# Hybrid decoder block on one Trainium2 core: block sums of the feed-forward input built with PSUM operands, the ones product four tiles into a unit, weight splits traced behind the norm factor, and the last stores on two queues

## The chip, the cores and the metric

The kernel runs on one core of one Trainium2 chip. The metric is the device time of one execution in microseconds (us). Three runs of the kernel before gave 2236.07, 2233.39 and 2236.08 us, median 2236.07 us. The core has a matrix engine (PE, with its weight loads shown as PEld), a vector engine (DVE), an activation engine (ACT), a general engine (POOL) and a queue engine (SP) that starts most DMA transfers. Each engine works through its own instructions strictly in order and waits on semaphores for the others.

## The reference, cut to what matters

One decoder layer over 1024 tokens and 1024 channels. The change touches the second half of it, the feed-forward block, and the norm ahead of it:

```python
        mixed = (...)                                  # three token mixers, merged by gates
        x = x + rms_norm(mixed @ w_out[l], post_mix_norm[l])
        h = rms_norm(x, pre_ffn_norm[l])               # (1, 1024, 1024)
        u = causal_dwconv(h @ ffn_w_up[l], ffn_conv_w[l], ffn_conv_b[l])   # 2 * 2816 columns, 3 taps
        gate, val = jnp.split(u, 2, axis=-1)
        f = (jax.nn.gelu(gate, approximate=True) * val) @ ffn_w_down[l]
        x = x + rms_norm(f, post_ffn_norm[l])
```

Everything is float32. `rms_norm(x, w)` is `x * rsqrt(mean(x*x) + 1e-6) * w` over the channels.

## The kernel before, in words

**Layout and precision.** Activations lie channel by token: a tile is 128 channels by 512 tokens, and the 1024 tokens form two halves, h = 0 and h = 1. Each float32 operand of a matmul is split into a rounded high part (an ACT copy) and the remainder, a low part (a subtraction on DVE or POOL). One product is three matmuls: high by high, high by low, low by high. A "unit" is 128 output channels for one half: 8 input tiles (k = 0..7) times three matmuls, 24 matmuls into one PSUM bank. PSUM has eight banks here: a pool `psd` of five for products (tile name `dense`) and a pool `psn` of three for everything else.

**Order.** A scheduler orders the instructions of each engine ahead of time by its own time model; what is traced earlier has precedence, and where the code says `keep_in_program_order` or `issue_after` the order is fixed by hand. On the chip each engine keeps that order, whatever arrives late.

**The output projection and the norm (L1334 to L1394).** For each half, eight units of `wo` are added to x and stored (L1363 to L1375). `finish` then makes the input of the feed-forward block: `rstd` (L1348) multiplies the sum of squares `osq` with a matrix of ones (two matmul records into `psn`), and ACT (Ln, Exp) and DVE turn it into a factor. Then eight tiles j are scaled by DVE (L1380), copied by ACT into the high part (L1383) and subtracted into the low part (L1389 on POOL for j = 1, 3, 5 of the second half, otherwise L1391 on DVE). For h = 0 this runs at once. For h = 1 it runs in the middle of the feed-forward block's first units.

**The first four pairs of units (N_FIRST = 4).** `up_first` (L1511) does the eight units u = 0..7 for h = 0. In the last pair (u = 6, 7) `fm_unit` (L273) calls `end` ahead of tile k = NORM_AT = 6 of unit 6: it traces the loads and splits of two further weights (`second`, for u = 0, 1 of the second half) and then `finish` for h = 1. The ones product and the first matmul of tile 6 are kept in program order; unit 7 is free to be put anywhere. The conv of these two units, the gelu (L1611) and the gated product (L1613) are held until tile j = SPLIT_AT = 5 of `finish` has been scaled and split.

`up_second` (L1528) does u = 0..7 for h = 1. For u = 0 and 1 the two units run interleaved tile by tile (L1531 to L1536), because the tiles of h = 1 come one after another out of `finish`. Every unit's weights are 512 KB by DMA into `wraw`, ACT makes the high part `whi` (L269), POOL the low part `wlo` (L270). Up to three such pairs of buffers take turns, so a unit's `whi` waits until the unit three before has been through PE. After each unit follows `conv` (L304): ACT L307 scales PSUM into `u`, ACT L311 does three halo columns, DVE L315 adds two taps; then gelu and, for each pair, the gated product L1503 and its store L1504.

**The block sums (L1577 to L1603).** From the fifth pair on, `up_pair` (L1548) uses a seven-product scheme over 2 by 2 blocks (weights in `weights7`, L1401). Its right-hand sides are sums and differences of the four blocks of h (halves 0 and 1, tiles k and k + 4). `columns` is a generator that `up_second` advances after each unit's conv. Its first four steps call `blocks(k)`: four DVE operations in place on SBUF tiles, `combos` (L1463 to L1466), and two splits (ACT L1591, DVE L1592); the last four steps make two splits each. That is 16 DVE instructions for sums and 16 for low parts. `up_pair` then runs the products in the order 1, 2, 6, 7, 5, 4, 3, each 12 matmuls.

**The end.** The last chunk of the down projection goes over columns 0:512, 512:768 and 768:1024 (`LAST`). `start_norm` (L1842) scales eight tiles by the last norm's factor (L1848), adds x (L1849, on POOL for some tiles, on DVE for the others) and stores each tile from SP (L1850).

Of the kernel before, what the change touches and what calls it, by code (L numbers as in the profile page):

```python
# [10 lines left out]
F32 = mybir.dt.float32  # L11
# [3 lines left out]
OP = mybir.AluOpType  # L15
# [170 lines left out]
SB_SLO = 1  # L186
SB_WLO = 0
H_POOL = (0, 1, 3, 5), (1, 3, 5)
SPLIT_AT = 5
NORM_AT = 6  # L190
T_POOL = (range(8), (0, 1, 2))

T_AT = 3
# [1054 lines left out]
def tail_stage(nc, tc, es, env):  # L1248
# [82 lines left out]
    ow = op.enter_context(tc.tile_pool(name="ow", reuse_waits="tile", bufs=2))  # L1331
    rows = []
    splits = []
    for h in range(2):  # L1334
        o = [x_t(F32) for _ in range(8)]
        rows.append(o)

        def sumsq(sums, src):

            if sums[0] is None:  # L1340
                sums[0] = ow.tile([128, 512], F32, name="osq", bufs=OSQ)
                act(sums[0], src, AF.Square)
            else:
                sq = psn.tile([128, 512], F32, name="psn", tag="psn")
                act(sq, src, AF.Square)
                V.tensor_tensor(sums[0], sums[0], sq, op=OP.add)

        def rstd(ss):  # L1348
            ss, = ss
            ps = psn.tile([128, 512], F32, name="psn", tag="psn")  # L1350
            tc.keep_in_program_order(mm(ps, E.ones, ss, start=True, stop=True))

            V.tensor_scalar(ss, ps, 1.0 / DM, EPS, op0=OP.mult, op1=OP.add)
            act(ps, ps, AF.Ln, scale=1.0 / DM, bias=E.eps)
            act(ps, ps, AF.Exp, scale=-0.5)
            V.tensor_tensor(ss, ss, ps, op=OP.mult)
            V.scalar_tensor_tensor(ss, ss, -0.5, ps, op0=OP.mult, op1=OP.mult)
            V.scalar_tensor_tensor(ps, ss, 1.5, ps, op0=OP.add, op1=OP.mult)
            return ps

        ss = [None]
        for j in range(8):
            ps, = fm_unit(psd, load_w3(A["wo"][j], 1024), lambda k, _: mix[h, k], 8, halves=(h,))  # L1363
            act(o[j], ps, AF.Copy)
            sumsq(ss, ps)
        r = rstd(ss)
        ss = [None]
        for j in range(8):
            x = ow.tile([128, 512], F32, name="ox", bufs=8)
            nc.sync.dma_start(x, A["xT"][j * 128:(j + 1) * 128, hs(h)])  # L1370
            p = psn.tile([128, 512], F32, name="psn", tag="psn")
            V.scalar_tensor_tensor(p, o[j], pvc(PV_PM, j), r, op0=OP.mult, op1=OP.mult)
            V.tensor_tensor(o[j], p, x, op=OP.add)
            sumsq(ss, o[j])
            nc.sync.dma_start(E.x1_d[j * 128:(j + 1) * 128, hs(h)], o[j])  # L1375
        def finish(h=h, o=o, ss=ss, rstd=rstd):
            r = rstd(ss)
            for j in range(9):
                if j < 8:
                    i = V.scalar_tensor_tensor(o[j], o[j], pvc(PV_FFN, j), r, op0=OP.mult, op1=OP.mult)  # L1380
                    tc.keep_in_program_order(i)
                    hi, lo = h2[h, j] = hi_t(), lo_t()
                    a = act(hi, o[j], AF.Copy)  # L1383
                    if j == SPLIT_AT:
                        splits[:] = a, i
                if j > 0:
                    hi, lo = h2[h, j - 1]
                    if j - 1 in H_POOL[h]:
                        P.tensor_tensor(lo, o[j - 1], fl(hi), op=OP.subtract)  # L1389
                    else:  # L1390
                        tc.keep_in_program_order(V.tensor_tensor(lo, o[j - 1], fl(hi), op=OP.subtract))  # L1391

        if h == 0:
            finish()  # L1394
# [63 lines left out]
        act(s, ps, AF.Copy)  # L1458
        return s

    def combos(b11, b12, b21, b22, eng):

        eng.tensor_tensor(b22, b12, b22, op=OP.subtract)  # L1463
        eng.tensor_tensor(b12, b11, b12, op=OP.subtract)
        eng.tensor_tensor(b11, b22, b11, op=OP.subtract)
        eng.tensor_tensor(b21, b11, b21, op=OP.add)  # L1466

    m_d = E.scratch("m_d", [NFF * 128, T])
    ms_d = [E.scratch(f"m{x}_d", [DOWN[-1][0] * 128, T]) for x in ("hi", "lo")]

# [40 lines left out]
    def up_first(f, st, ending=False):  # L1511
        us = 2 * f, 2 * f + 1
        ws = [load_up(u, 0) for u in us]

        def end():
            second.extend(load_up(u, 1) for u in range(2))
            finish()

        for s, u in enumerate(us):
            ps, = fm_unit(psd, ws[s], lambda k, h: h2[h, k], 8, halves=(0,),  # L1520
                          at=(NORM_AT, end) if ending and s == 0 else None)
            with ExitStack() as after:
                if ending:
                    for i in splits:
                        after.enter_context(tc.issue_after(i.ins))
                conv(u, 0, ps, st, gelu=False)

    def up_second(f, st, then):  # L1528
        us = 2 * f, 2 * f + 1
        if f == 0:  # L1530
            pss = [bank() for _ in us]  # L1531
            for k in range(8):
                for (hi, lo), ps in zip(second, pss):
                    s = slice(k * 128, (k + 1) * 128)
                    for n, (a, b) in enumerate(((hi, 0), (hi, 1), (lo, 0))):
                        mm(ps, a[:, s], h2[1, k][b], start=k == 0 and n == 0, stop=k == 7 and n == 2)  # L1536
        for s, u in enumerate(us):
            if f:
                ps, = fm_unit(psd, load_up(u, 1), lambda k, h: h2[h, k], 8, halves=(1,))
            else:  # L1540
                ps = pss[s]
            end = conv(u, 1, ps, st)
            if s == 1:
                gated(f, 1, st)
            with tc.issue_after(end.ins):
                then(u)
# [30 lines left out]
    rhs = {q: [None] * 4 for q in range(1, 8)}  # L1577
    sums = {}

    def blocks(k):  # L1580
        lows = [rows[0][k], rows[1][k], rows[0][k + 4], rows[1][k + 4]]
        combos(*lows, V)
        for q, b in ((1, h2[0, k]), (2, h2[0, k + 4]), (3, h2[1, k + 4])):
            rhs[q][k] = b
        t2, t1, t4, t3 = lows
        sums.update({(6, k): t2, (7, k): t3, (5, k): t1, (4, k): t4})

    def split(q, k, place):
        t = sums[q, k]
        rhs[q][k] = hi, lo = place(), x_t()  # L1590
        act(hi, t, AF.Copy)  # L1591
        V.tensor_tensor(lo, t, fl(hi), op=OP.subtract)  # L1592

    def columns():
        for k in range(4):
            blocks(k)
            split(6, k, x_t)
            split(7, k, x_t)
            yield
        for q, k, place in ((5, 0, hi_t), (5, 2, hi_t), (4, 0, lo_t), (4, 2, lo_t)):  # L1600
            split(q, k, place)
            split(q, k + 1, place)
            yield  # L1603

    first = [{} for _ in range(N_FIRST)]
# [184 lines left out]
    ws = []  # L1790
# [51 lines left out]
    def start_norm(h, s, ss):  # L1842
# [3 lines left out]
        for j in range(8):  # L1846
            a = acc[h][j][:, s]
            V.tensor_tensor(a, a, r[:, :W], op=OP.mult)  # L1848
            (P if j in T_POOL[end] else V).tensor_tensor(a, x1s[h][:, j, s], a, op=OP.add)  # L1849
            nc.sync.dma_start(E.outT[j * 128:(j + 1) * 128, h * 512 + s.start:h * 512 + s.stop], a)  # L1850

    for s0, s1 in LAST:
        h = s0 // 512
# [40 lines left out]
```

## Time and profile before

| What | Before |
|---|---|
| Median of three runs | 2236.07 us (2233.39 to 2236.08) |
| The profiled execution's own time | 2236.53 us |
| Its span, first to last instruction | 2234.8 us |
| PE busy, share of span | 2158.0 us, 97% |
| PEld busy | 1748.4 us, 78% |
| DVE busy | 1361.1 us, 61% |
| ACT busy | 1262.5 us, 56% |
| POOL busy | 1091.7 us, 49% |
| Granted PE clock, mean | 0.988 |
| DMA moved | 240.73 MB, mean 108 GB/s |

Times inside the profile count from the start of the span. A row of the timeline gives start, duration, engine, source line, operation, output and inputs, and in brackets the idle time of the engine just before and what ended it. A window row gives the length of a stretch, then for each engine its busy time and the number of its instruction records in it, then the granted PE clock, the DMA share and GB/s. Successive instructions of an engine overlap a little, so a duration is somewhat larger than the step from one start to the next. Some matmul records are missing from a trace. All matmuls carry line L205, the wrapper that issues them.

### The profile page before, as it was taken

The numbers are of one execution on the slowest core, as the hardware profiler recorded it, in microseconds if no ns is written. First come the engines' busy times: TensorE is split into PE (matmuls) and PEld (weight loads), VectorE is DVE, ScalarE is ACT, GpSimd is POOL, SyncE is SP. The second block draws the span as 40 slices with busy tenths as digits, with TensorE's granted clock in tenths as the row PEclk, the third lists the DMA queues.
The fourth block names the chain that finished last, engine by engine and source line by source line (L and its number), as shares of the span: only waits on it lengthen the run. The fifth ranks groups of instructions, "written<-read, shape, count | busy, mean of one in ns | idle before, by whom it ended". The sixth has DMA issues, their size and how long they took to land.

```text
span 2234.8 us, 30188 instructions
## 1 busy us (share of the span) xinstructions
PE 2158.0 (97%) x10697; PEld 1748.4 (78%) x10697; DVE 1361.1 (61%) x2538; ACT 1262.5 (56%) x2316; POOL 1091.7 (49%) x797
## 2 busy tenths in 40 slices
PE   8999999999999999999999999999989999999997
PEld 7997667667887878777777788888768888888886
DVE  8433784771367677848484443328785666666677
ACT  7144676666476677545555422235556666676574
POOL 3212566576233323434343246445467777765753
PEclk9999999999999999999999999999989999999998
DMA  5223212201111111322223263345334444476533
GB/s 197 83 82 104 57 34 79 64 8 46 49 48 43 53 47 43 113 81 90 95 76 118 78 225 131 106 135 179 118 99 161 160 151 146 141 264 201 186 108 110
DMA packets 127079, 240.73 MB, mean 108 GB/s; under 512 B 29328, under 2 KB 43472, under 8 KB 126928
## 3 DMA queue, kind: packets, MB, share of 16 engines
q1 hardware_dynamic: 126640, 238.58, 32.6%
q8 instruction: 84, 1.38, 0.3%
q14 instruction: 67, 0.55, 0.1%
q10 hardware_dynamic: 288, 0.22, 0.0%
HBM read 179.45 MB, written 59.31 MB: 107 GB/s over the span
## 4 chain that ended last, share of the span: by engine, by line
PE 85%; DVE 8%; ACT 3%; issue 2%; DMA 1%; POOL 1%; SPq 0%; DVEq 0%; ACTq 0%; POOLq 0%
PE dense L205 67%; PE ps_s L205 6%; PE ps_o L205 6%; PE ps_t L205 5%; PE ps_b L205 2%; DVE x L1592 1%; DVE dec L1160 1%; DVE mx L838 0%; DVE x L1848 0%; DVE row L530 0%; ACT wT L862 0%; DVE row L1225 0%; POOL wT_lo L873 0%; ACT h_hi L401 0%; DVE sz L1043 0%
## 5 line engine op out<-in xcount | busy, mean ns | idle before, releaser
L270 POOL TENSOR_TENSOR wlo<-wraw,whi 128x1024 fp32r<-128x1024 f32 (+1 forms) x118 | 270.0, 2290 | 425.7 <-ACT whi L269 423.4
L205 PE MATMUL dense<-h_hi,whi 128*128 128x512 f32 x992 | 400.4, 404 | 10.0 <-DVE row L530 6.3
L205 PE MATMUL dense<-h_hi,wlo 128*128 128x512 f32 x992 | 388.9, 392 | 0.0
L205 PE MATMUL dense<-h_lo,whi 128*128 128x512 f32 x992 | 388.8, 392 | 0.0
L269 ACT ACTIVATE whi<-wraw 128x1024 fp32r<-128x1024 f32 (+1 forms) x118 | 117.9, 999 | 200.6 <-PE dense L205 173.5
L205 PEld LDWEIGHTS dense<-h_hi,whi 128*128 128x128 f32 x992 | 187.4, 189 | 51.1 <-issue 6.6
L205 PEld LDWEIGHTS dense<-h_hi,wlo 128*128 128x128 f32 x992 | 186.7, 188 | 40.7 <-issue 0.8
L205 PEld LDWEIGHTS dense<-h_lo,whi 128*128 128x128 f32 x992 | 187.4, 189 | 34.8 <-issue 0.2
L873 POOL TENSOR_TENSOR wT_lo<-wT,wT_hi 128x512 fp32r<-128x512 f32 x132 | 168.8, 1289 | 87.1 <-ACT wT_hi L872 78.3
L205 PE MATMUL dense<-hi,whi 128*128 128x512 f32 x512 | 201.0, 396 | 8.9 <-ACT whi L1412 4.8
L205 PE MATMUL dense<-lo,whi 128*128 128x512 f32 x512 | 201.7, 394 | 0.3 <-DVE lo L1391 0.3
L205 PE MATMUL dense<-hi,wlo 128*128 128x512 f32 x512 | 199.8, 393 | 0.5 <-POOL wlo L1413 0.4
L1073 POOL TENSOR_TENSOR s_lo<-sa,s_hi 128x512 fp32r<-128x512 f32 (+2 forms) x48 | 53.9, 1126 | 150.7 <-ACT s_hi L1072 141.6
L205 PEld LDWEIGHTS dense<-hi,whi 128*128 128x128 f32 x512 | 97.2, 190 | 31.7 <-ACT whi L1412 5.3
L205 PE MATMUL dense<-x,uhi 128*128 128x512 f32 x360 | 116.7, 389 | 0.0
L205 PEld LDWEIGHTS dense<-hi,wlo 128*128 128x128 f32 x512 | 97.1, 190 | 22.4 <-POOL wlo L1413 1.1
L862 ACT ACTIVATE wT<-ps_s 128x512 f32<-128x512 f32 x132 | 78.5, 595 | 63.6 <-PE ps_s L205 59.2
L205 PEld LDWEIGHTS dense<-lo,whi 128*128 128x128 f32 x512 | 97.2, 190 | 21.8 <-issue 0.7
L315 DVE SCALAR_TENSOR_TENSOR u<-dense,pv,u 128x510 f32<-128x510 f32 (+1 forms) x140 | 101.7, 742 | 8.7 <-ACT u L311 7.5
L872 ACT ACTIVATE wT_hi<-wT 128x512 fp32r<-128x512 f32 x132 | 82.3, 629 | 16.6 <-POOL wT L864 15.1
L205 PE MATMUL ps_s<-Q,K 128*128 128x512 f32 x264 | 83.6, 398 | 4.3 <-DVE Q L849 4.1
L205 PEld LDWEIGHTS dense<-x,uhi 128*128 128x128 f32 x360 | 67.6, 188 | 14.1
(460 smaller groups left out, 5631.9 us busy)
## 6 DMA issues: line engine op xcount, KB each, us to landing
wraw<-in_wfm SPq DMA_DIRECT2D x62, 512.0 KB, 3.7
wraw<-in_wup SPq DMA_DIRECT2D x52, 512.0 KB, 3.8
g_d<-gate_e SPq DMA_DIRECT2D x48, 256.0 KB, 2.0
ge<-g_d SPq DMA_DIRECT2D x24, 512.0 KB, 3.9
m_d<-u SPq DMA_DIRECT2D x44, 256.0 KB, 2.1
u<-m_d SPq DMA_DIRECT2D x36, 256.0 KB, 3.3
wraw<-in_wdn SPq DMA_DIRECT2D x33, 256.0 KB, 3.4
cum<-acum_d SPq DMA_DIRECT2D x32, 256.0 KB, 3.3
```

Of the source, the lines that this page charges most:

```text
L205: i = f(*a, **k)
L269: act(hi, raw, AF.Copy)
L270: (eng or (V if tiles else P)).tensor_tensor(lo, raw, fl(hi), op=OP.subtract)
L315: end = V.scalar_tensor_tensor(o[:, d:], ps[:, :512 - d], taps[d], o[:, d:], op0=OP.mult, op1=OP.add)
L862: act(w.rearrange("p h q -> p (h q)"), pz, AF.Exp)
L872: act(hi, wf, AF.Copy)
L873: P.tensor_tensor(lo, wf, fl(hi), op=OP.subtract)
L1073: (P if SB_SLO else V).tensor_tensor(s_lo[:, c0:], a[:, c0:], fl(s_hi[:, c0:]), op=OP.subtract)
L1160: V.tensor_scalar(dec[:, h, :], cum[:, h, :], E.acum[:, c, 4 * q + h:4 * q + h + 1], 0.0, op0=OP.subtract, op1=OP.min)
L1592: V.tensor_tensor(lo, t, fl(hi), op=OP.subtract)
```

## The change

Four edits; all but the two-queue stores lie between the output projection and the first seven-product pair.

1. `blocks` copies the block b12 into a PSUM tile by ACT (`in_psum`, L1445) and forms two of the four sums in PSUM tiles of `psn`; each of the four DVE operations now has one PSUM input. The splits for products 7 and 6 read those PSUM tiles. For products 5 and 4 each sum is first copied to PSUM by ACT, and the split reads the copy. The fourth operation stays an addition (`b21 = t2 + b21`).
2. The ones product of `finish` for h = 1 is traced at tile 4 of unit 6, not 6, and unit 7 is issued behind it.
3. The two weight loads of `second` with their splits are traced behind the factor (`then` is called after `rstd`), and the conv, gelu and gated product of the last first-half pair are held until tile 7, not 5.
4. The interleaved units 0 and 1 of the second half run tile by tile for k = 0 to 4 only; then unit 0 does k = 5 to 7, and then unit 1. In the last `start_norm` odd tiles are stored from ACT's queue, even ones from SP's.

```diff
-SPLIT_AT = 5
-NORM_AT = 6
+SPLIT_AT = 7
+NORM_AT = 4
...
-            tc.keep_in_program_order(mm(ps, E.ones, ss, start=True, stop=True))
+            summed[0] = mm(ps, E.ones, ss, start=True, stop=True)
+            tc.keep_in_program_order(summed[0])
...
-        def finish(h=h, o=o, ss=ss, rstd=rstd):
+        def finish(h=h, o=o, ss=ss, rstd=rstd, then=None):
             r = rstd(ss)
+            if then:
+                then()
...
         def end():
-            second.extend(load_up(u, 1) for u in range(2))
-            finish()
+            finish(then=lambda: second.extend(load_up(u, 1) for u in range(2)))
 
         for s, u in enumerate(us):
-            ps, = fm_unit(psd, ws[s], lambda k, h: h2[h, k], 8, halves=(0,),
-                          at=(NORM_AT, end) if ending and s == 0 else None)
+            with ExitStack() as after:
+                if ending and s:
+                    after.enter_context(tc.issue_after(summed[0].ins))
+                ps, = fm_unit(psd, ws[s], lambda k, h: h2[h, k], 8, halves=(0,),
+                              at=(NORM_AT, end) if ending and not s else None)
...
-            for k in range(8):
-                for (hi, lo), ps in zip(second, pss):
-                    s = slice(k * 128, (k + 1) * 128)
-                    for n, (a, b) in enumerate(((hi, 0), (hi, 1), (lo, 0))):
-                        mm(ps, a[:, s], h2[1, k][b], start=k == 0 and n == 0, stop=k == 7 and n == 2)
+            for k, s in [(k, s) for k in range(5) for s in range(2)] + [(k, s) for s in range(2) for k in range(5, 8)]:
+                hi, lo = second[s]
+                c = slice(k * 128, (k + 1) * 128)
+                for n, (a, b) in enumerate(((hi, 0), (hi, 1), (lo, 0))):
+                    mm(pss[s], a[:, c], h2[1, k][b], start=k == 0 and n == 0, stop=k == 7 and n == 2)
...
     def blocks(k):
-        lows = [rows[0][k], rows[1][k], rows[0][k + 4], rows[1][k + 4]]
-        combos(*lows, V)
+        b11, b12, b21, b22 = rows[0][k], rows[1][k], rows[0][k + 4], rows[1][k + 4]
...
-        t2, t1, t4, t3 = lows
-        sums.update({(6, k): t2, (7, k): t3, (5, k): t1, (4, k): t4})
+        p, t3, t2 = in_psum(b12), psn_t(), psn_t()
+        V.tensor_tensor(t3, p, b22, op=OP.subtract)
+        V.tensor_tensor(b12, b11, p, op=OP.subtract)
+        V.tensor_tensor(t2, t3, b11, op=OP.subtract)
+        V.tensor_tensor(b21, t2, b21, op=OP.add)
+        split(7, k, x_t, t3)
+        split(6, k, x_t, t2)
+        sums.update({(5, k): b12, (4, k): b21})
...
         for q, k, place in ((5, 0, hi_t), (5, 2, hi_t), (4, 0, lo_t), (4, 2, lo_t)):
-            split(q, k, place)
-            split(q, k + 1, place)
+            for m in (k, k + 1):
+                split(q, m, place, in_psum(sums[q, m]))
...
-            nc.sync.dma_start(E.outT[j * 128:(j + 1) * 128, h * 512 + s.start:h * 512 + s.stop], a)
+            (nc.scalar if end and j % 2 else nc.sync).dma_start(
+                E.outT[j * 128:(j + 1) * 128, h * 512 + s.start:h * 512 + s.stop], a)
```

`split(q, k, place, t)` now takes its source t as an argument; `psn_t()` takes a tile of the pool `psn`.

More of the change, by code (lines that the diff above doesn't have):

```diff
@@ L1333, in tail_stage @@
     splits = []
+    summed = [None]
     for h in range(2):
@@ L1459, in snap @@
         return s
[L1461 to L1466, printed above, removed]
     m_d = E.scratch("m_d", [NFF * 128, T])
@@ L1578, in tail_stage, with psn_t, split @@
     sums = {}
+    def psn_t():
+        return psn.tile([128, 512], F32, name="psn", tag="psn")
     def blocks(k):
-        lows = [rows[0][k], rows[1][k], rows[0][k + 4], rows[1][k + 4]]
-        combos(*lows, V)
+        b11, b12, b21, b22 = rows[0][k], rows[1][k], rows[0][k + 4], rows[1][k + 4]
         for q, b in ((1, h2[0, k]), (2, h2[0, k + 4]), (3, h2[1, k + 4])):
             rhs[q][k] = b
-        t2, t1, t4, t3 = lows
-        sums.update({(6, k): t2, (7, k): t3, (5, k): t1, (4, k): t4})
-    def split(q, k, place):
-        t = sums[q, k]
+        p, t3, t2 = in_psum(b12), psn_t(), psn_t()
[6 more added lines that the diff above has]
+        sums.update({(5, k): b12, (4, k): b21})
+    def split(q, k, place, t):
         rhs[q][k] = hi, lo = place(), x_t()
@@ L1596, in columns @@
             blocks(k)
-            split(6, k, x_t)
-            split(7, k, x_t)
             yield
         for q, k, place in ((5, 0, hi_t), (5, 2, hi_t), (4, 0, lo_t), (4, 2, lo_t)):
-            split(q, k, place)
-            split(q, k + 1, place)
+            for m in (k, k + 1):
+                split(q, m, place, in_psum(sums[q, m]))
             yield
```

## The prediction, made before the changed kernel ran

> **What bounds the kernel now.** I read the page first, then the chain of waits, then windows over the stretch where the chain leaves PE.
>
> ```profile
> span 2234.8 us, 30188 instructions
> ```
> ```profile
> 1579.35 2.90 PE dense L205 x13
> ...
> 1585.89 1.20 DVE lo L1391
> ...
> 1587.13 16.88 PE dense L205 x66
> ...
> 1645.35 8.88 DVE x L1592 x5
> ...
> 1660.57 318.22 PE dense L205 x1392
> ```
>
> The span is 2234.8 us, and the same execution took 2236.53 us, so 1.7 us lie around it and 0.46 us separate it from the median of 2236.07. Before 1582 us and from 1660.57 us on, for 318 us, the chain is matmuls only: there nothing but fewer matmuls would help. In between it passes to the norm (DVE L1391) and to the splits of the block sums (DVE L1592). That stretch, in windows (length, then PE, PEld, DVE, ACT, POOL busy with their record counts, then the PE clock):
>
> ```profile
> 1582.64:1585.91 3.27, 0.16 (x2) 0.01 (x1) 3.13 (x6) 1.72 (x3) 3.27 (x2) 1.00 0.21 48
> 1585.91:1590.64 4.73, 4.47 (x11) 3.28 (x12) 4.66 (x7) 2.66 (x5) 3.53 (x3) 0.64 0.54 191
> ...
> 1604.50:1607.50 3.00, 1.95 (x6) 0.89 (x6) 0.00 (x0) 3.00 (x5) 2.74 (x2) 1.00 0.00 0
> 1607.50:1633.80 26.30, 26.29 (x116) 21.40 (x114) 25.58 (x25) 14.55 (x32) 18.32 (x9) 1.00 0.33 112
> 1633.80:1638.64 4.84, 0.00 (x1) 0.01 (x1) 4.84 (x8) 2.54 (x5) 0.16 (x1) 0.97 0.43 153
> 1638.64:1645.60 6.96, 6.59 (x16) 4.72 (x17) 5.79 (x7) 6.96 (x13) 5.62 (x3) 0.53 0.35 114
> ...
> 1655.90:1660.57 4.67, 0.07 (x1) 0.00 (x0) 4.63 (x5) 1.31 (x3) 3.75 (x3) 0.81 0.35 104
> 1660.57:1666.00 5.43, 5.43 (x13) 4.28 (x14) 2.25 (x5) 2.51 (x5) 0.00 (x0) 0.53 0.68 199
> ```
> ```profile
> 1667.86 0.39 PE L205 MATMUL dense<-x,uhi 128*128 128x512 f32 x1
> ...
> 1671.26 0.39 PE L205 MATMUL dense<-hi,uhi 128*128 128x512 f32 x1
> ```
>
> Fifteen matmuls start between 1667.86 and 1671.26, so one costs 0.227 us at full clock. Against that pace four gaps lose time, each counted with the slow clock (0.53 to 0.64) behind it:
> - A, 1582.64 to 1590.64: 8.00 us for 11 matmuls (2.5 us). Lost 5.5.
> - B, 1604.50 to 1607.50: 3.00 us for 6 (1.4). Lost 1.6.
> - C, 1633.80 to 1645.60: 11.80 us for 17 (3.9). Lost 7.9.
> - D, 1655.90 to 1666.00: 10.10 us for 14 (3.2). Lost 6.9.
>
> Together 21.9 us. As a check by work: eight units and five products (252 matmuls, 57.2 us) took the 77.9 us from 1582.64 to 1660.57, which is 20.7, and 13 matmuls (3.0 us) took the next 5.43, which is 2.5; so 23.2. The difference is lost records; I take 21.9.
>
> **Edit 1, block sums from PSUM.** Here is what DVE did from 1590 to 1660:
>
> ```profile
> L1592 DVE TENSOR_TENSOR x<-x 128x512 fp32r<-128x512 f32 x8 | 8.4, 1067 | 0.0
> L1592 DVE TENSOR_TENSOR x<-x,lo 128x512 fp32r<-128x512 f32 x4 | 7.9, 2039 | 0.0
> ...
> L1592 DVE TENSOR_TENSOR x<-x,hi 128x512 fp32r<-128x512 f32 x4 | 6.8, 1734 | 0.0
> L1464 DVE TENSOR_TENSOR x<-x 128x512 f32<-128x512 f32 x4 | 4.9, 1232 | 0.0
> L1463 DVE TENSOR_TENSOR x<-x 128x512 f32<-128x512 f32 x4 | 4.8, 1197 | 0.0
> L1465 DVE TENSOR_TENSOR x<-x 128x512 f32<-128x512 f32 x4 | 3.8, 958 | 0.0
> L1466 DVE TENSOR_TENSOR x<-x 128x512 f32<-128x512 f32 x4 | 3.8, 956 | 0.0
> ```
> ```profile
> 1628.82 1.74 POOL L1419 TENSOR_TENSOR uf<-uf,wraw 128x512 f32<-128x512 f32 x1
> ```
> ```profile
> 1629.33 1.78 DVE L1592 TENSOR_TENSOR x<-x 128x512 fp32r<-128x512 f32 x1
> ```
> ```profile
> L1719 DVE TENSOR_TENSOR u<-psn,u x6: 681/681/684, 2043.3 to 2126.7; 128x512 f32<-128x512 f32 x6
> ```
> ```profile
> 2042.93 1.31 POOL L1663 TENSOR_TENSOR vlo<-vf,vhi 128x512 fp32r<-128x512 f32 x1
> ```
> ```profile
> L1722 DVE TENSOR_TENSOR psn<-psn,u x8: 690/693/700, 2004.2 to 2130.3; 128x512 f32<-128x512 f32 x8
> ```
>
> The 32 instructions took 23.1 us (L1592) and 17.3 us (L1463 to L1466), 40.4 us together. Their inputs are all in SBUF, and beside a POOL subtraction one takes 1.78 us. The down stage has the same operations with one PSUM input, beside a POOL that splits weights there too (L1663 at 2042.93 beside the first L1719 at 2043.3): 0.68 to 0.70 us, without one slow case. 32 at 0.69 are 22.1 us, so DVE is relieved of 18.3 us. DVE was busy for 25.58 of the 26.30 us ahead of gap C and lags PE; C and D lose 14.8 us together, less than the relief. What comes late next in C and D is ACT:
>
> ```profile
> 1634.54 0.63 ACT L1591 ACTIVATE x<-x 128x512 fp32r<-128x512 f32 x1 [4.43 <-DVE x L1592]
> ...
> 1637.55 1.04 ACT L1412 ACTIVATE whi<-wraw 128x1024 fp32r<-128x1024 f32 x1
> ```
> ```profile
> L1447 ACT ACTIVATE psn<-u x42: 572/597/697, 2000.1 to 2174.3; 128x512 f32<-128x512 f32 x42
> ```
>
> ACT had waited 4.43 us for DVE with the next weights' high part (L1412) queued behind. That wait goes. Added are 12 copies to PSUM at 0.60, 7.2 us of ACT; it was busy for 14.55 of the 26.30 us, so they lie beside PE. Uncovered they would cost 7.2 us. The pool `psn` has three tiles and one block takes all three, so the copy of the next block waits for the splits of this one; that chain is 8 steps of about 0.65, 5.2 us, against 24 matmuls or 5.4 us of PE per unit: just covered, and the products need the last sums only five units later. I take C and D as closed but for 1.5 us (bounds 0 and 8: at worst the weights are still queued behind a wait and one of the two gaps stays).
>
> **Edits 2 and 3, the ones product and what it waits for.**
>
> ```profile
> 1573.36 0.68 DVE L1346 TENSOR_TENSOR osq<-osq,psn 128x512 f32<-128x512 f32 x1
> ```
> ```profile
> 1578.33 1.02 PE L205 MATMUL psn<-osq,ones 128*128 128x512 f32 x2
> ```
> ```profile
> 1580.11 0.66 ACT L1354 ACTIVATE psn<-psn,eps 128x512 f32<-128x512 f32 x1 [6.86 <-DVE osq L1353]
> 1580.70 1.05 ACT L269 ACTIVATE whi<-wraw 128x1024 fp32r<-128x1024 f32 x1
> 1581.65 0.59 ACT L1355 ACTIVATE psn<-psn 128x512 f32<-128x512 f32 x1
> ```
>
> ```profile
> 1581.82 4.70 POOL L270 TENSOR_TENSOR wlo<-wraw,whi 128x1024 fp32r<-128x1024 f32 x2 [7.42 <-ACT whi L269]
> ```
>
> The sum of squares was ready at 1574.04, the ones product started at 1578.33, and only 13 matmuls stood behind it. From its end at 1579.35 to the first low part at 1587.09 passed 7.7 us, with 0.95 us of weight split between Ln and Exp. Now four tiles of unit 6 and all of unit 7 come behind it: 36 matmuls, 8.2 us. PE ran out at 1582.64 (the 0.16 us in the first window is the tail of the last matmul); less the 8.2 and the ones product's 1.02 it now reaches the ones product at 1573.4 and waits 0.6 us. The low part is there 7.7 less 0.95, or 6.8 us, after its end, ahead of the 8.2; without these 36 matmuls as cover it would cost the 6.8 us. So gap A closes, for 0.6 us of new wait: a gain of 4.9 us (bounds: 2 if the split still slips between and DVE is slow, 5.5). What is queued behind the ones product on PE is all of unit 7, and with it everything; DVE and ACT behind it wait too. The two moved weight splits issue two DMAs on SP, whose loads landed long before; their low parts take POOL 2.35 us each, against 5.4 us of PE per unit.
>
> Holding conv, gelu and gated product to tile 7 costs two PSUM banks for some microseconds longer; units u = 0, 1, 2 use the other three, so nothing waits.
>
> **Edit 4.** Unit 0 of the second half ends nine matmuls (2.0 us) earlier, so the high part of unit 3's weights, which waits for its buffer, can start under matmuls. Gap B falls from 1.6 to about 0.5 us (bounds 0 and 1.6).
>
> The end of the kernel:
>
> ```profile
> 2228.89 1.76 DVE L1849 TENSOR_TENSOR x<-x,x 128x256 f32<-128x256 f32 x5
> ```
> ```profile
> 2230.74 1.38 SPq L1850 DMA_DIRECT2D out_dram<-x  x3
> ```
>
> DVE is done at 2230.65, the last store ends its issue on SP at 2232.12, after three issues in 1.38 us. ACT has no work left there. On two queues the last store follows its addition directly, with one issue of about 0.46 us: it ends at 2231.1, 1.0 us earlier. I take 0.9 us (bounds 0, if the transfers themselves hold the end, and 1.2).
>
> The slow clock behind the gaps is part of the sum: 11 matmuls in 4.73 us, 16 in 6.96 and 13 in 5.43, at clocks of 0.64, 0.53 and 0.53, are 17.1 us where 40 at 0.227 take 9.1; so 8.0 of the 21.9 us. The Trainium skill's page TensorE: Matmul & The Clock Gate, section Part 1: The HAM clock gate, gives half clock until about 3.4 us of activity have passed, after an idle window of as much; by that estimate three slow stretches cost 1.7 us each, 5.1, which makes the gain 2.9 us smaller and the time 2218.8 us. The trace shows half clock too, but for 4.7 to 7 us; the rows decide.
>
> **The sum.** Gains: A 4.9, B 1.1, C and D 13.3, stores 0.9; together 20.2 us. From 2236.53 that is 2216.3, as a median 0.46 lower: 2215.9 us.
>
> **The rivals.**
> - *One of the late gaps stays.* The order is fixed by a time model ahead of the run, ACT's queue is one, and the copies add to it; the weights of the first seven-product pair can still come late. For it: the 4.43 us wait above had exactly this form. Against it: DVE no longer lags. Price: gap C's 7.9 us on top of the forecast; 2223.8 us.
> - *Only the norm gap closes.* If the PSUM inputs free DVE but the chain through three `psn` tiles takes its place, C and D stay: 4.9, 1.1 and 0.9 gained, 2229.2 us. Against it: 5.2 us of chain per 5.4 us unit.
> - *No change.* The stage gets shorter, but the later pairs' weights are not there earlier and PE waits then for what it waited for before. Against it: 318 us of matmuls follow without a break, so their weights had some lead. About 2236 us.
> - *Slower, ACT becomes the bound.* The 12 copies come on top of a queue in which weight splits stand behind sums; if ACT has no slack, the gaps stay and 7.2 us come on top: 2243 us. It decides if ACT's work per unit exceeds 5.4 us; 14.55 us busy in 26.30 with 7.2 more is 21.8, so against.
>
> **How the numbers follow.** A change of 0.2%, about what a measurement of this kernel can tell from no change, is 4.5 us. Forecast (A to D nearly closed, 2212 to 2219) 0.55; one late gap stays 0.25; only the norm gap 0.09; no change 0.05; slower 0.06. The range: low end all gaps by the higher count (23.2 less 0.6) and 1.2 at the end, 23.8 us below 2236.07, so 2212; high end 2228, past the second case and towards the third, leaving about 2 in 10 outside. Faster 0.89, same 0.05, slower 0.06.
>
> **What would show it.** Right: the ones product near 1574; no PE idle of over 1 us between it and the first seven-product pairs; the splits at about 0.69 us each; DVE below 80% where it was full; the granted clock at 1.00 through the stage; the 0.95 us between Ln and Exp gone; two queues storing at the end. Wrong: PE idle with ACT's `psn` copies or weight splits as the releaser; splits still at 1.7 us; a stall behind the ones product; new gaps in the 318 us that follow.

## The result

The changed kernel took 2213.42 us (median of 4 runs, 2211.36 to 2215.56), the kernel before 2236.07 beside it (4 runs, 2233.39 to 2236.79). The ratio is 0.9901, 95% interval 0.9884 to 0.9918: 22.65 us or 1.0% faster. The prediction was 2215.9, range 2212 to 2228. The profiled execution took 2215.56 us, its granted clock was 0.992 on average, where before's was 0.988. From the page of the changed kernel (span, and busy time by engine):

```profile
span 2213.7 us, 30202 instructions
...
PE 2151.5 (97%) x10697; PEld 1744.6 (79%) x10697; DVE 1340.3 (61%) x2538; ACT 1266.6 (57%) x2328; POOL 1087.1 (49%) x797
```

The shares of the whole span hardly move; the stage tells it. First what PE waited for between 1560 and 1700 us (total, times, longest), before and then after:

```profile
PE dense L205 <- ACT whi L1412: 4.8, 1, 4.8
PE dense L205 <- ACT psn L1447: 4.6, 1, 4.6
PE dense L205 <- ACT hi L1383: 3.1, 1, 3.1
PE dense L205 <- ACT whi L269: 0.9, 1, 0.9
PE dense L205 <- POOL wlo L1413: 0.4, 1, 0.4
PE dense L205 <- DVE lo L1391: 0.3, 1, 0.3
```
```profile
PE psn L205 <- DVE osq L1347: 0.4, 1, 0.4
```

Gaps A (`hi`, `lo`), B (`whi` L269), C (`whi` L1412, `wlo`) and D (`psn`) are all gone, 14.1 us of plain waiting and the slow clock behind them. One short wait is new: the ones product for the sum of squares. The chain of the changed kernel passes from that product to matmuls without a break, 82.82 us of them up to 1660 us, where this view ends:

```profile
1576.24 1.12 PE psn L205 x2
1577.37 82.82 PE dense L205 x365
```

The windows of the changed kernel over the first gap and over the stretch of B, C and D; the clock column reads 1.00 in both. The second stretch in the kernel before stands behind it, PE busy for 59.70 us and DVE for 63.01 (90%):

```profile
1582.64:1590.64 8.00, 8.00 (x37) 6.60 (x37) 7.92 (x12) 5.18 (x9) 6.26 (x4) 1.00 0.31 78
...
1590.00:1660.00 70.00, 70.00 (x310) 57.94 (x309) 52.78 (x83) 58.95 (x110) 46.87 (x27) 1.00 0.42 139
```
```profile
1590.00:1660.00 70.00, 59.70 (x244) 47.03 (x242) 63.01 (x68) 41.80 (x77) 42.61 (x21) 0.94 0.25 84
```

DVE is at 52.78 of 70.00, 75%, and ACT at 58.95, 84%, the busiest of the helpers now, and still not full. The groups of DVE from 1585 to 1655 in the changed kernel (busy, mean ns of one, idle time before):

```profile
L1598 DVE TENSOR_TENSOR x<-psn,x 128x512 fp32r<-128x512 f32 x8 | 5.4, 680 | 0.6 <-ACT x L1597 0.6
...
L1598 DVE TENSOR_TENSOR x<-psn,hi 128x512 fp32r<-128x512 f32 x4 | 2.8, 690 | 3.2 <-ACT hi L1597 3.2
L1587 DVE TENSOR_TENSOR psn<-psn,x 128x512 f32<-128x512 f32 x4 | 2.8, 689 | 0.0
L1589 DVE TENSOR_TENSOR psn<-psn,x 128x512 f32<-128x512 f32 x4 | 2.7, 685 | 0.0
L1590 DVE TENSOR_TENSOR x<-psn,x 128x512 f32<-128x512 f32 x4 | 2.7, 682 | 0.0
L1588 DVE TENSOR_TENSOR x<-x,psn 128x512 f32<-128x512 f32 x4 | 2.7, 674 | 0.0
L1598 DVE TENSOR_TENSOR x<-psn,lo 128x512 fp32r<-128x512 f32 x4 | 2.6, 682 | 0.3 <-ACT lo L1597 0.3
```

The 32 instructions take 21.7 us, where they took 40.4.

**A clock that starts at the same place.** Two profiled executions do not reach this stage at the same moment. In both kernels the same code leads up to the ones product ahead of the one in question (the output projection's own norm, second half). It started at 1544.77 us before, and 2.16 us later after. From the timelines of PE and DVE, before and then after:

```profile
1544.77 1.02 PE L205 MATMUL psn<-osq,ones 128*128 128x512 f32 x2
```
```profile
1546.93 1.02 PE L205 MATMUL psn<-osq,ones 128*128 128x512 f32 x2
...
1644.56 0.39 PE L205 MATMUL dense<-lo,ahi 128*128 128x512 f32 x1
...
2208.99 1.76 DVE L1853 TENSOR_TENSOR x<-x,x 128x256 f32<-128x256 f32 x5
```

So the traces are compared by the stretch from there to the end of the span: 690.03 us before, 666.77 after, 23.26 less. It splits at the first matmul of product 4 (before: 1660.57, where gap D ended) and at the end of DVE's last addition (before: 2230.65; after: 2210.75). Up to product 4: 115.80 and 97.63 us, 18.17 less. The order of the products is not quite the same: PE has 425 records up to that point in the changed kernel and 416 before, so nine more matmuls, 2.0 us at 0.227, lie ahead of it. For the same work it is about 20.2 us less. From there to the last addition: 570.08 and 566.19, 3.89 less, or about 1.9 for the same work; the slow clock behind gap D lies there. Behind the last addition: 4.15 and 2.95, 1.20 less. How well such a stretch repeats can be seen in the table below: four kernels whose only wait of PE in the stage is the 0.4 us for the sum of squares (the changed kernel, weight splits ahead, units interleaved, and stores on one queue less the 1.4 us that its end is longer) lie between 666.0 and 666.8, so differences under about 0.8 us say nothing.

### The profile page after: what moved, and what is told of

Its sections match the earlier page's. It is cut to its first block, busy times and chain, and to the rows that moved or that the text cites. A ratio compares the mean times of both kernels' runs of the same rounds, so it can differ in the third digit from the quotient of the medians.

```text
span 2213.7 us, 30202 instructions
## 1 busy us (share of the span) xinstructions
PE 2151.5 (97%) x10697; PEld 1744.6 (79%) x10697; DVE 1340.3 (61%) x2538; ACT 1266.6 (57%) x2328; POOL 1087.1 (49%) x797
## 4 chain that ended last, share of the span: by engine, by line
PE 87%; DVE 7%; ACT 2%; issue 2%; DMA 1%; POOL 1%; SPq 0%; DVEq 0%; ACTq 0%; POOLq 0%
PE dense L205 69%; PE ps_s L205 6%; PE ps_o L205 6%; PE ps_t L205 5%; PE ps_b L205 2%; DVE mx L838 1%; DVE dec L1160 1%; DMA wraw<-in_wdn 0%; DVE x L1852 0%; DVE row L530 0%; ACT wT L862 0%; DVE row L1225 0%; POOL wT_lo L873 0%; DMA cum<-acum_d 0%; DVE sz L1043 0%
## 5 line engine op out<-in xcount | busy, mean ns | idle before, releaser
L270 POOL TENSOR_TENSOR wlo<-wraw,whi 128x1024 fp32r<-128x1024 f32 (+1 forms) x118 | 269.5, 2285 | 419.5 <-ACT whi L269 417.3
L269 ACT ACTIVATE whi<-wraw 128x1024 fp32r<-128x1024 f32 (+1 forms) x118 | 117.9, 1000 | 202.3 <-PE dense L205 175.8
L315 DVE SCALAR_TENSOR_TENSOR u<-dense,pv,u 128x511 f32<-128x511 f32 (+1 forms) x140 | 101.9, 740 | 5.4 <-ACT u L311 4.2
L205 PEld LDWEIGHTS dense<-x,uhi 128*128 128x128 f32 x360 | 67.6, 188 | 14.1
```

The source lines that it names most:

```text
L205: i = f(*a, **k)
L269: act(hi, raw, AF.Copy)
L270: (eng or (V if tiles else P)).tensor_tensor(lo, raw, fl(hi), op=OP.subtract)
L315: end = V.scalar_tensor_tensor(o[:, d:], ps[:, :512 - d], taps[d], o[:, d:], op0=OP.mult, op1=OP.add)
```

## The experiments

The theory: what was slow on DVE was two SBUF inputs beside a POOL that reads SBUF; edit 1 takes that away and closes C and D, the ones product with 36 matmuls kept behind it closes A. The rivals: the parts are worth something only together, the tile order (edit 4) or the place of the weight splits (edit 3) carries it, or POOL has nothing to do with DVE's slow cases. All runs in one table. "Stretch" is the one just defined, from one profile each; the ratio is to the kernel before, measured beside it (medians 2236.07 to 2236.22).

| Kernel | Median us | Ratio, 95% interval | Third ones product, span end | Stretch |
|---|---|---|---|---|
| before | 2236.07 | 1 | 1544.77, 2234.8 | 690.03 |
| after | 2213.42 | 0.9901 [0.9884, 0.9918] | 1546.93, 2213.7 | 666.77 |
| edit 1 alone | 2221.19 | 0.9930 [0.9913, 0.9946] | 1544.21, 2218.8 | 674.59 |
| all but edit 1 | 2232.51 | 0.9979 [0.9970, 0.9989] | 1545.36, 2230.9 | 685.54 |
| POOL does not read (before) | 2219.51 | 0.9917 [0.9903, 0.9932] | 1543.65, 2214.7 | 671.05 |
| ones product at tile 6 | 2217.43 | 0.9912 [0.9897, 0.9927] | 1544.68, 2216.1 | 671.42 |
| unit 7 free | 2217.54 | 0.9914 [0.9899, 0.9928] | 1544.27, 2215.8 | 671.53 |
| ones product at tile 5 | 2216.19 | 0.9906 [0.9892, 0.9921] | 1543.68, 2212.2 | 668.52 |
| hold to tile 5 | 2215.90 | 0.9907 [0.9891, 0.9924] | 1545.10, 2213.7 | 668.60 |
| weight splits ahead | 2214.15 | 0.9902 [0.9888, 0.9917] | 1545.99, 2212.0 | 666.01 |
| units interleaved to the end | 2214.96 | 0.9904 [0.9889, 0.9919] | 1546.68, 2213.3 | 666.62 |
| stores on one queue | 2213.30 | 0.9897 [0.9881, 0.9914] | 1544.25, 2211.7 | 667.45 |
| last norm in PSUM | 2213.31 | 0.9897 [0.9882, 0.9912] | 1543.25, 2208.3 | 665.05 |
| last norm in `psn` | 2212.34 | 0.9890 [0.9875, 0.9905] | 1545.12, 2210.8 | 665.68 |

### Edit 1 alone, and all but edit 1

The kernel before with the new `blocks` only:

```diff
-        lows = [rows[0][k], rows[1][k], rows[0][k + 4], rows[1][k + 4]]
-        combos(*lows, V)
...
+        p, t3, t2 = in_psum(b12), psn_t(), psn_t()
+        V.tensor_tensor(t3, p, b22, op=OP.subtract)
...
-            split(q, k, place)
-            split(q, k + 1, place)
+            for m in (k, k + 1):
+                split(q, m, place, in_psum(sums[q, m]))
```

> The kernel before with edit 1 alone (block sums and splits with a PSUM input). Theory: the late gaps C and D (14.8 us with their slow clock) come from DVE operations with two SBUF inputs that are held up beside POOL; with a PSUM input each takes 0.69 us, C and D close, gaps A and B and the stores stay as they are: 2236.1 less 13 to 15, so 2221 to 2223 us. Rival 1: C and D come from the late end of the interleaved first two units (1604 us), not from DVE's speed; then at most 4 us are gained, 2232 us or more. Rival 2: ACT, with 12 more copies, becomes the bound: 2236 to 2243 us.

And the changed kernel with the same lines turned back:

> The changed kernel with the block sums and their splits put back on SBUF tiles; all other edits stay. Theory: gaps A and B stay closed and the stores stay fast, but the splits take 1.0 to 2.0 us beside POOL again; since the stage begins earlier for DVE by some 8 us, part of its lag is made up: 6 to 15 us slower than 2213.4, so 2219 to 2228 us. Rival 1 (the early start is what closes C and D): 2213 to 2216 us, although the splits are slow.

Edit 1 alone gave 15.0 us in the median (15.4 by the stretch), as its theory had it; both of its rivals fell. The waits of PE that it left are A and B, as they were:

```profile
PE dense L205 <- ACT hi L1383: 3.1, 1, 3.1
...
PE dense L205 <- ACT whi L269: 0.9, 1, 0.9
```

The other three edits without it gave 3.7 us (4.5 by the stretch), less than expected. A and B are gone, but C and D are still there, C has grown from 4.8 to 5.8, and a wait of 1.8 us for a weight's low part (POOL `wlo` L270, at 1613.46) is new. Waits of PE and a group of DVE in that kernel:

```profile
PE dense L205 <- ACT whi L1416: 5.8, 1, 5.8
...
PE dense L205 <- ACT psn L1451: 3.8, 1, 3.8
...
PE dense L205 <- POOL wlo L270: 1.8, 1, 1.8
```
```profile
L1598 DVE TENSOR_TENSOR x<-x 128x512 fp32r<-128x512 f32 x8 | 10.3, 1294 | 0.0
```

Where DVE sets the pace, much of what PE gains by arriving sooner goes into a longer wait for DVE. So the parts do not add up: 15.4 and 4.5 are 19.9, together they are 23.3. Edits 2 to 4 are worth 7.8 us once DVE is relieved (674.59 less 666.77), and 4.5 while it lags.

### POOL does not read

The kernel before; POOL fills the weights' low parts and sums of this stage with zeros in place of computing them, so it still writes SBUF and no longer reads it. DVE's instructions are those of before, with both inputs in SBUF.

```diff
+    def low(dst, f):
+        return P.memset(fl(dst) if dst.dtype == R32 else dst, 0.0) if E.still[0] else f()
...
-        P.tensor_tensor(u1, a21, a22, op=OP.add)
+        low(u1, lambda: P.tensor_tensor(u1, a21, a22, op=OP.add))
```

> The kernel before in which POOL, from the second half's third unit to the sixth pair, fills the low parts and the sums of the weights with zeros in place of subtracting and adding (left out: these low parts and sums). POOL then reads nothing from SBUF there. Theory (held up by POOL's reads): the in-place sums and the splits take 0.68 us although both inputs stay in SBUF, and C and D close as with PSUM inputs: 2221 to 2224 us. Rival (the operations are slow for their own two SBUF reads, or any POOL instruction holds them up): splits stay at 1.0 to 2.0 us, 2232 us or more.

DVE's groups in that kernel, and then one stretch of the timeline, POOL's fills beside DVE's splits:

```profile
L1601 DVE TENSOR_TENSOR x<-x 128x512 fp32r<-128x512 f32 x8 | 5.2, 678 | 0.0
...
L1601 DVE TENSOR_TENSOR x<-x,lo 128x512 fp32r<-128x512 f32 x4 | 2.5, 689 | 0.0
```
```profile
1618.25 1.47 POOL L1407 MEMSET uf<- 128x512 f32 x3 [4.48 <-PE dense L205]
```
```profile
1618.74 1.28 DVE L1601 TENSOR_TENSOR x<-x 128x512 fp32r<-128x512 f32 x2
```

With both inputs in SBUF and POOL only writing beside them, the splits take 0.68 us, where the same instructions took 1.07 and 2.04. No split was slow: all 16 lie between 0.674 and 0.693 us. C, D and B went, and the time fell by 16.7 us (19.0 by the stretch); of PE's waits in the stage only A stayed, 3.1 us as before. Behind it, though, the clock stayed at 1.00 here: 21 matmuls in 4.71 us, where 11 took 4.73 at 0.64 before. So about 2.2 of the 19.0 us are the clock and not DVE. The wait, and the window behind it:

```profile
PE dense L205 <- ACT hi L1388: 3.1, 1, 3.1
```
```profile
1584.79:1589.50 4.71, 4.71 (x21) 3.79 (x22) 4.63 (x8) 3.15 (x6) 2.60 (x2) 1.00 0.41 161
```

So POOL's reading was the cause, not the SBUF inputs as such. The Trainium skill's page SBUF — State Buffer, section Who interferes with whom, says that a DVE instruction with two SBUF inputs contends with a GpSimd instruction that reads SBUF, and not with one that only writes it; this trace agrees, with 0.68 us beside fills. One thing goes along with the cause here: the fills are also shorter than the subtractions, so the weights' low parts were ready sooner. That bears on the time of the run, not on the 0.68 us of a split beside a fill.

### What stands behind the ones product

Three kernels, each the changed one but for these lines. Ones product at tile 6 and unit 7 free to go ahead of it; at tile 4 and unit 7 free; at tile 5.

```diff
-NORM_AT = 4
+NORM_AT = 6
...
-                if ending and s:
-                    after.enter_context(tc.issue_after(summed[0].ins))
```

> The changed kernel with the ones product back at tile 6 and unit 7 free to go ahead of it. Theory: gap A returns, 4 to 6 us with its slow clock, and nothing else, since DVE has slack behind it: 2217 to 2219.5 us; PE idle of about 2 to 3 us behind the ones product. Rival: the norm's chain is short enough once the weight split is out of it and two blocks of work lie behind it; then less than 2 us, 2213 to 2215 us.

```diff
-                if ending and s:
-                    after.enter_context(tc.issue_after(summed[0].ins))
```

> The changed kernel, but the matmuls of the unit that holds the ones products are not tied to the order behind them: 21 of them go ahead of the ones products, and 15 are left behind, 3.4 us, where 6.7 us are needed. The ones products are issued at tile 4 as before. Theory: what closed the gap at the norm is the number of matmuls that stand behind the ones products, so most of it comes back: TensorE waits about 3 us for the first low part, and the time is near 2216.5 to 2217.5, as with the ones products at tile 6. Rival: the place of the ones products in the program sets it and not what stands behind them: no wait, and 2213 to 2214.

```diff
-NORM_AT = 4
+NORM_AT = 5
```

> The ones products of the norm stand behind tile 5 of the unit and not behind tile 4: 33 matmuls of 0.2269 us are left behind them, 7.5 us, where the first low part came 6.7 us after them in the changed kernel. Theory: the 0.4 us that TensorE waits for the sum of squares goes, the cover still holds, and no other wait comes: from the third ones product to the end 666.3 to 667, a time within 0.5 us of the changed kernel. Rival: the last 0.8 us of cover isn't enough, since the chain behind the ones products also waits for ScalarE's other work: a wait of 1 to 3 us and a time of 2214.5 to 2216.5.

The waits of PE in the stage, at tile 6, with unit 7 free, and at tile 5:

```profile
PE dense L205 <- ACT hi L1387: 3.1, 1, 3.1
...
```
```profile
PE dense L205 <- ACT hi L1387: 2.3, 1, 2.3
PE dense L205 <- POOL lo L1393: 0.9, 1, 0.9
PE dense L205 <- POOL wlo L270: 0.4, 1, 0.4
```
```profile
PE dense L205 <- ACT whi L269: 1.1, 2, 0.9
PE dense L205 <- DVE lo L1395: 0.4, 1, 0.4
```

At tile 6 gap A is back with its full 3.1 us (4.65 by the stretch). With unit 7 free the program still says tile 4, but the ones product starts at 1577.82, 33.55 us behind the third one, as in the kernel before (33.56), and not 29.31 as in the changed kernel. 3.6 us of waits and 4.8 us by the stretch come back: the 36 matmuls kept behind the product are the edit, its place in the program alone gains nothing (the wait for the high part is 0.8 us shorter than at tile 6, but 1.3 us of waits for low parts came in). At tile 5 the wait for the sum of squares went, as the theory had it, and the cover held: the first low part was ready 6.4 us behind the ones product, under 7.5 us of matmuls. The 0.4 us came at 1585.71, for a later low part, which took 2.48 us on DVE while POOL was splitting a weight (L270, 1582.70 to 1585.11):

```profile
1583.17 2.48 DVE L1395 TENSOR_TENSOR lo<-x,hi 128x512 fp32r<-128x512 f32 x1 [1.29 <-ACT hi L1387]
```

1.1 us more were for `whi` L269 near 1600, gap B again: 1.75 us worse by the stretch. So it is the rival's time, but not the rival's mechanism: the cover was not too short.

### Hold, weight splits and tile order

The last two heads' hold back to tile 5, the weights traced ahead of `finish`, and the two units interleaved to the end:

```diff
-SPLIT_AT = 7
+SPLIT_AT = 5
```

> The hold on the activations' splits of the last two heads ends at tile 5 and not at tile 7, as it did in the kernel before. Theory: the norm's two inputs (the addition of the squares and the two activations behind the ones product) still go ahead, since they are issued at tile 4; the other head's tiles are split earlier beside them, so at most 1 us changes: from the third ones product (the output projection's second one) to the end of the span 666.0 to 668, after: 666.8. Rival: the splits that come earlier stand ahead of the norm on VectorE and ScalarE, and the first low part comes later than the products that cover it: a wait of TensorE of 1 to 3 us near 1580, and a time near 2215 to 2216.

```diff
-            finish(then=lambda: second.extend(load_up(u, 1) for u in range(2)))
+            second.extend(load_up(u, 1) for u in range(2))
+            finish()
```

> The changed kernel with the two weight loads and splits traced ahead of the norm's factor again. Theory: a split slips between Ln and Exp at most (0.95 us), and the 36 matmuls behind the ones product cover that (low part 6.7 us after its end now, 7.7 then, against 8.2): PE idle stays under 0.5 us, 2213 to 2214 us. Rival: the split delays the first tile past the cover and brings slow clock with it: 1 to 4 us, 2214.4 to 2217.5 us.

```diff
-            for k, s in [(k, s) for k in range(5) for s in range(2)] + [(k, s) for s in range(2) for k in range(5, 8)]:
+            for k, s in [(k, s) for k in range(8) for s in range(2)]:
```

> The changed kernel with units 0 and 1 of the second half interleaved through all eight tiles. Theory: unit 0 ends up to 2 us later, the weights of the unit that waits for its buffer come late as in gap B, 0.5 to 1.9 us of PE idle near 1604: 2214 to 2215.5 us. Rival (gap B came only from the late tiles of the norm, which put the third unit's matmuls ahead): no idle of PE there, 2213.4 us.

The hold seems to be worth a little: with tile 5 gap B is back (below), at 1601.74, and the stretch is 1.8 us longer, of which that wait explains half; where the rest went is not shown. The time is the rival's, the place is not (the rival's was near 1580); the intervals of the two ratios overlap.

```profile
PE dense L205 <- ACT whi L269: 0.9, 1, 0.9
```

The weight splits traced ahead changed nothing (666.01 against 666.77), and the timeline of ACT in that kernel shows why: the split stands behind both norm activations there too.

```profile
1577.89 0.58 ACT L1357 ACTIVATE psn<-psn 128x512 f32<-128x512 f32 x1
1579.05 1.06 ACT L269 ACTIVATE whi<-wraw 128x1024 fp32r<-128x1024 f32 x1 [0.58 <-PE dense L205]
```

It waits for its buffer, which PE gives back only then. The run with the ones product at tile 6 shows the opposite case: the weights were still traced behind the factor, and yet the split slipped in ahead of the second activation:

```profile
1580.61 1.05 ACT L269 ACTIVATE whi<-wraw 128x1024 fp32r<-128x1024 f32 x1
1581.56 0.59 ACT L1357 ACTIVATE psn<-psn 128x512 f32<-128x512 f32 x1
```

So tracing the ones product at tile 4 took the split out (with unit 7 free it was out as well), and the trace order of the weights did not. And the tile order bought nothing: with the units interleaved to the end, PE runs through from the ones product for 72 us, past 1604, and the stretch is 666.62. There the rival held and the theory fell, although the median, 2214.96, lies in the theory's range. The order does bring the weight split in question forward (it ends 23.9 us behind the ones product after, 24.4 us with the units interleaved to the end), but PE waits for it in neither.

```profile
1577.12 72.08 PE dense L205 x317
```

### The end of the kernel

All last stores on SP's queue, and two tries to go further, with the squares of the last norm (and the temporary of its reciprocal root) in PSUM: in the banks of the products, and in the norms' own pool.

```diff
-            (nc.scalar if end and j % 2 else nc.sync).dma_start(
+            nc.sync.dma_start(
```

> The changed kernel with all last stores from SP's queue. Theory: in the profile the end, from DVE's last addition to the end of the span, grows from 2.95 back to 4.15 us, and nothing else changes: 2213.4 plus 1.2, so 2214.6 us (within what the runs scatter, so the profile decides). Rival (the transfers hold the end, not their issue): 2.95 us stays.

```diff
-        rt, v = [fw.tile([128, 4], F32, name=f"r{x}", bufs=2) for x in "tv"]
+        rt, v = fw.tile([128, 4], F32, name="rt", bufs=2), bank()
...
-                sq = up_.tile([128, 512], F32, name="snap", bufs=5)
+                sq = bank()
```

> The changed kernel with the same idea put to the last norm: the squares are written to PSUM in place of SBUF, and so is the temporary of the reciprocal root, so that the eight additions and the three small operations have one SBUF input beside POOL's additions. Theory: in the last chunk the additions fall from about 1.2 to 0.4 us and the small ones from 0.4 and 0.65 to 0.16 us; the sum of squares is then bound by PE's last matmul, 1.8 us earlier, and the chain of small ones is 1.1 us shorter: 2.9 us, 2210.5 us. Rival (ACT's squares and PE's last matmuls set that chain, or POOL's additions, now later, do): 0 to 1 us, 2212.4 to 2213.4 us.

```diff
-        rt, v = [fw.tile([128, 4], F32, name=f"r{x}", bufs=2) for x in "tv"]
+        rt, v = fw.tile([128, 4], F32, name="rt", bufs=2), ps[:, 8:12]
...
-                sq = up_.tile([128, 512], F32, name="snap", bufs=5)
+                sq = psn.tile([128, 512], F32, name="psn", tag="psn")
```

> The last norm's squares go to a PSUM buffer of the norms' own pool and not to SBUF, and its reciprocal root to columns of its sums' tile; the run that put them into the products' own banks made VectorE's additions for that norm three times as fast and gained nothing in the median, with about 4 us of new waits of TensorE for those banks. Theory: the gain is there if the products' banks are left alone: no wait of TensorE behind the squares of the last norm above 1 us, and a time 2 to 3 us below the changed kernel, 2210.5 to 2211.5. Rival: the three buffers of the norms' pool are too few, the squares wait for one another, and TensorE waits for them as it did for the products' banks: 2213 to 2216.

On one queue DVE's last addition ends at 2207.34 (below) and the span at 2211.7, 4.36 us later, against 2.95 on two: 1.4 us in the profile, as the theory had it, and not to be told in the medians (2213.30 and 2213.42).

```profile
2205.58 1.76 DVE L1853 TENSOR_TENSOR x<-x,x 128x256 f32<-128x256 f32 x5
```

The two tries moved the wait. L1841 is ACT's copy of the norm's factor, the last of the chain of small operations; L1876 is DVE's addition of the squares. In the changed kernel PE waited mostly for the first. The waits of PE near the end in the changed kernel, with the squares in the products' banks, and with them in `psn`:

```profile
PE psn L205 <- ACT u L1841: 6.4, 2, 3.9
PE psn L205 <- DVE u L1876: 0.4, 1, 0.4
```
```profile
PE psn L205 <- ACT u L1841: 3.2, 3, 1.7
PE dense L205 <- DVE u L1876: 2.2, 2, 1.9
PE psn L205 <- DVE u L1876: 2.0, 1, 2.0
```
```profile
PE psn L205 <- DVE u L1876: 4.8, 1, 4.8
PE psn L205 <- ACT u L1841: 3.3, 2, 1.7
```

The chain of small operations got shorter, as the theory had it (6.4 to 3.2 and 3.3 us), and what ACT's line loses, DVE's line gains: 6.8, 7.4 and 8.1 us in sum. The stretch is 1.7 and 1.1 us shorter, the medians are 2213.31 and 2212.34, both inside the changed kernel's own runs. The squares in `psn` do queue for its tiles, as the rival had it (one waited 2.0 us for DVE's scaling, L1852), with a time between the theory's and the rival's; whether a microsecond is left is open. No version here beats the changed kernel by more than its runs scatter.

## Why the prediction was right

The sign, the size and the mechanism of the two large terms (A, and C with D) were right; the gain was 22.65 us by the medians and 23.26 by the stretch, where the sum had 20.2. The reasons given for two small steps, the split between the two activations and gap B, were wrong. Point by point:

- **Edit 1, DVE.** Forecast 0.69 us each and 22.1 us for 32; measured 0.67 to 0.69 and 21.7. The nearest row (the down stage's instruction with one PSUM input beside a reading POOL) carried it, and the run with POOL's reads taken away shows the cause. (The POOL instruction shown beside the slow split, L1419, adds weights and does not subtract; the reading stands.)
- **C and D.** Counted at 14.8 lost; edit 1 alone gave 15.4 by the stretch. The 1.5 us left over in the forecast was too careful: nothing is left. The 12 added copies hid: ACT was busy for 58.95 of 70.00 us, and no wait of PE in the stage ends at one.
- **A.** The wait at the ones product: forecast 0.6, measured 0.4. First low part behind its end: forecast 6.8; measured 1584.08 less 1577.36 is 6.7, under 8.2 us of cover. The low part alone took 1.02 us of it, with both inputs in SBUF and beside a POOL split that had started at 1581.12. From DVE's timeline of the changed kernel:

```profile
1583.06 1.02 DVE L1395 TENSOR_TENSOR lo<-x,hi 128x512 fp32r<-128x512 f32 x1
```

  Putting the product back cost 4.65 us, where the forecast took 4.9. The 0.95 us between the two activations went, but not by the trace order of the weights (edit 3), as the step had it; tracing the ones product at tile 4 did that. That the step's gain came all the same was luck.
- **B.** Forecast 0.5 us left, by the tile order. It is gone, and this step failed in its reason: with the tile order turned back it stayed away, and with the tile order in place it came back at tile 5 (both the hold and the ones product). What of the stage's order decides it is not settled; the wait is always that for `whi` L269. Here too the gain came by luck.
- **Stores.** Forecast 0.9, measured 1.2 (1.4 with the queue turned back), in the profile alone.
- **The count of the gaps.** 21.9 by gap, 23.2 by work. The stretch less the stores gained 22.1, and 0.4 of new wait is in it, so 22.5 were lost: between the two. The waits listed for the stage before (14.1) and the slow clock by the prediction's rows (8.0) make 22.1, much the same. The 252 matmuls of the check by work are the right number, but not for the reason given: PE ran product 4 ahead of product 5 in both traces, and the fifth product counted is one of the next pair's, taken forward. The difference to the forecast, 3.1 us, is so 1.5 (C and D), 0.5 (B), 0.2 (the new wait), 0.3 (stores) and 0.6 (the count).
- **The slow clock.** By the rows the slow stretches cost 8.0 us, and 21.9 were lost in all. By the estimate from the Trainium skill's page TensorE: Matmul & The Clock Gate, section Part 1: The HAM clock gate, they cost 5.1, which would make it 19.0. The measured 22.5 goes with the rows.
- **The rivals.** None held for the whole change. The run without edit 1 gained 3.7 us, between "no change" and "only the norm gap closes" (6.9): there C and D stayed, and C grew.

The sum treated each gap as one edit's own. That was safe only because all edits came together.

## What to carry to other kernels

Look at the same instruction's duration in another stage: here a DVE operation that took 0.68 us in one place and 2.0 in the next was held up by POOL's reads, and a PSUM operand, or a POOL that didn't read at that time, gave the difference back. A matrix product that starts a long chain on other engines wants enough independent matmuls fixed behind it, counted against the chain (36 for 6.7 us here); moving it earlier in the program without fixing them gained nothing. Relieve the engine that lags first: while DVE lagged, closing the other gaps gave 4.5 us of the 7.8 that it gave afterwards.

## What the runs showed of the hardware

- POOL pays for the contention too. A 128x512 sum of weights (L1419 before, L1423 after) took 1.74 us in the stage of before, 1.31 us here, and 1.30 with edit 1 alone; POOL's group from 1590 to 1660 in the changed kernel:

```profile
L1423 POOL TENSOR_TENSOR uf<-uf,wraw 128x512 f32<-128x512 f32 x3 | 3.9, 1306 | 0.0
```

- The place of a second input costs nothing by itself: 0.674 to 0.690 us with one input in PSUM, 0.678 to 0.690 with both in SBUF where POOL only writes.
- The same gap of 3.1 us at the norm was followed by a slow clock in three profiles (before and edit 1 alone 0.64, ones product at tile 6 0.71) and by none in the one in which POOL does not read (1.00). A gap of 0.9 us (B, before) and one of 2.3 us (unit 7 free) left the clock at 1.00 in the window behind. What decides it is not shown; the slow clock behind a gap of this size is not a fixed price.
- The same code up to the third ones product took between 1543.25 and 1546.93 us over the 14 profiles, 3.7 us apart. Differences of 1 to 2 us behind it could be read only from a common point in the trace.
